# A half copy put behind all products of an up-projection tile, and accumulating transfers queued in threes

## The chip, the cores and the metric

The kernel runs on one core of one Trainium2 chip. The metric is the device time of one execution in microseconds. The kernel before took 2319.51 us (median of 3 runs, 2316.69 to 2325.53). All profile lines come from one further execution, which took 2328.08 us, 0.4% above that median.

## What is computed

A two-layer decoder trunk on one sequence of 256 rows of 2048 numbers, in float32. Each layer is a mixer (a short gated convolution, then stick-breaking attention) and an MLP, each with a norm before and after. The change lies in the MLP, which both layers have, with a hidden width of 8192:

```python
def sq_relu_mlp(u, w_up, w_down):
    return jnp.square(jax.nn.relu(u @ w_up)) @ w_down

for i in range(DEPTH):                       # DEPTH = 2
    ...
    u = rmsnorm(h, mlp_pre_g[i])
    h = h + rmsnorm(sq_relu_mlp(u, mlp_w_up[i], mlp_w_down[i]), mlp_post_g[i])
```

## The kernel before

**Two parts of each number.** The kernel's matmuls take operands of type float32r, so every float32 operand is split in two: a rounded high part (ScalarE, L163 or L208, tile `whi`) and what is left of it (VectorE, L174, tile `wlo`). A product of two numbers is made of three of the four products of the parts. Weights arrive in chunks of 128 x 1024 (512 KB) in four `raw` buffers (L147, issued by SyncE's queue), and the split parts lie in rings of seven `hi` and seven `lo` buffers. A `raw` buffer is loaded again when VectorE has made the low part of its chunk.

**The up projection.** A tile is 128 of the hidden columns for all 256 rows. It is summed in one PSUM bank of 512 columns. `high` (L899) makes 16 products of a weight's high part with both parts of `u`, 512 columns each: the first 256 columns of the bank hold high times high, the last 256 hold high times low. `half_of` (L910) then copies the last 256 columns to SBUF on ScalarE (L912, tile `half`). `low` (L914) makes 16 products of the weight's low part with the high part of `u`, 256 columns each, into the first 256 columns of the same bank. `finish` (L921) calls `Hidden.tile` (L857): VectorE adds `half` to the first 256 columns (L859, tile `s`), ScalarE takes relu and square (L860, L861), and the result is split for the next projection (L247/L248 or L842/L843).

**The order of the two projections.** The hidden width is cut into 8 steps of 8 tiles. `lead_up` (L924) makes the 8 tiles of the first step: six of them side by side, product by product, in banks 2 to 7, then two one after the other (`whole_up`, L946). From then on one tile of the next step (`whole_up`, always in bank 2, `UP_BANK`) takes turns with one pair of tiles of the down projection of this step (`Down.pair`, L1012). There are 56 such turns in each layer: 7 steps, each of two halves of four turns (m = 0 to 3).

**The down projection.** The pairs m = 1, 2, 3 of a half use a scheme with seven products in place of eight (`seven`, L1029: 21 matmuls of 512 columns, L1008 to L1010, in banks 3, 4, 5 and 6, 7, 0, 1). Its extra sums of weights are made by VectorE (L200) and of the hidden part by VectorE (L882). The pair m = 0 uses eight products (`eight`, L1040: 24 matmuls): first six into bank 3, six into bank 4, then six into bank 2, the bank of the up tile just before it, then six into bank 5. The bank-2 part is added to the result at once (L959 on ScalarE the first time, L961 on VectorE later), and the next up tile takes bank 2 again.

**Joints.** A `Down` object covers four turns at the start and eight turns after that, so there are seven joints in each layer at which one ends and the results leave PSUM: VectorE adds banks 3, 4 and 5 to the results (L961), and `add_later` (L965) copies banks 6, 7, 0 and 1 into a staging tile `more` (ScalarE, L969) and issues nine accumulating transfers of 256 KB each from SBUF to SBUF on GpSimd's queue (L975). Some of the nine depend on others: `r[0,1]`, `r[1,0]` and `r[1,1]` take several sums one after the other.

**What sets the order.** TensorE runs in the order of the code. A scheduler orders ScalarE, VectorE, GpSimd and SyncE by the program's order and its own estimate of when inputs are ready; each of these engines then runs strictly in that built order. `chunk` (L229) has weights split four chunks ahead of their use. Dependencies inside a PSUM bank are kept for the whole tile: a copy that reads the last 256 columns and a matmul that writes the first 256 are ordered one behind the other.

Of the kernel before, what the change touches and what calls it, by code (L numbers as in the profile page):

```python
# [9 lines left out]
F32 = mybir.dt.float32  # L10
F32R = mybir.dt.float32r
AF = mybir.ActivationFunctionType
ALU = mybir.AluOpType

P = 128
D = 2048
T = 256
NB = T // P
KD = D // P
# [67 lines left out]
def trunk(ctx, tc, x, xT, vecs, rows, ws, out):  # L87
    nc = tc.nc
# [30 lines left out]
    def bank(i, name):  # L119
        return psum.tile([P, 512], F32, tag=f"b{i}", name=name)  # L120
# [108 lines left out]
    def chunk(i, low=True):  # L229
        while count["split"] <= min(i + (AHEAD if i >= CALM else 2), len(stream) - 1, max(i, count["limit"])):  # L230
            split_one()
        if low:
            low_parts(i)
        return parts[i]
# [36 lines left out]
    def spent(us):  # L271
        clock["us"] += us
        while due and due[0][0] <= clock["us"]:
            heappop(due)[2]()
# [559 lines left out]
    def mlp(pool, i, before, after):  # L834
# [56 lines left out]
                two_parts(more, t[:, P:])  # L891
                return [one] + [[m[:, j * P : (j + 1) * P] for m in more] for j in range(3)]

        pss, halves = {}, {}

        def weight(part, first, m):
            return chunk(first + m // CH, part == 1)[part][:, m % CH * P : (m % CH + 1) * P]

        def high(first, m, k, n, number, b=None):  # L899

            if n not in pss:
                pss[n] = bank(number, "up")
            ps, x = pss[n][:].rearrange("p (a b t) -> p a b t", a=2, b=NB), u[k // 4][:, k % 4]
            if b is None:
                nc.tensor.matmul(ps, weight(0, first, m), x, start=k == 0, stop=k == KD - 1)  # L905
            else:
                nc.tensor.matmul(ps[:, :, b, :], weight(0, first, m), x[:, :, b, :], start=k == 0 and b == 0, stop=False)
            spent(TILE_HIGH if b is None else TILE_LOW)

        def half_of(n):  # L910
            halves[n] = pool.tile([P, T], F32, tag="half", name="half", bufs=2)
            nc.scalar.activation(halves[n][:], pss[n][:, T:], AF.Copy)  # L912

        def low(first, m, k, n):  # L914
            x = u[k // 4][:, k % 4, 0].rearrange("p b t -> p (b t)")
            nc.tensor.matmul(  # L916
                pss[n][:, :T], weight(1, first, m), x, start=False, stop=k == KD - 1, skip_group_check=True
            )
            spent(TILE_LOW)

        def finish(to, n):  # L921
            to.tile(n, pss.pop(n), halves.pop(n))

        def lead_up(to):  # L924
            first = W["mlp", i, 0].base
            place = {kn: m for m, kn in enumerate(UP_FIRST)}
            lead = list(range(LEAD_UP))
            alone = [(k, n) for k in range(ALONE) for n in lead]
            for b in range(NB):
                for k, n in sorted(alone, key=lambda kn: (kn[0] // 4, kn[1] // 3 if kn[0] < 4 else 0)):  # L930
                    high(first, place[k, n], k, n, n + 2, b)
            for k, n in alone:
                low(first, place[k, n], k, n)
            for k in range(ALONE, KD):
                for n in lead:
                    high(first, place[k, n], k, n, n + 2)
                for n in lead:
                    if k == KD - 1:
                        half_of(n)
                    low(first, place[k, n], k, n)  # L940
                    if k == KD - 1:
                        finish(to, n)
            for n in range(LEAD_UP, NF):
                whole_up(to, n, first + 2 * n, (n + 2) % 8)

        def whole_up(to, n, first, number):  # L946
            for k in range(KD):
                high(first, k, k, n, number)
            half_of(n)
            for k in range(KD):  # L950
                low(first, k, k, n)
            finish(to, n)
# [12 lines left out]
        def add_later(j, p1, p5, p6, p7):  # L965
            t = pool.tile([P, 4, 512], F32, tag="gpost", name="more", bufs=1)
            t1, t5, t6, t7 = (t[:, m, :] for m in range(4))
            for to, ps in ((t1, p1), (t6, p6), (t5, p5), (t7, p7)):
                nc.scalar.activation(to, ps[:], AF.Copy)  # L969
            r = {(b, c): part[b][2 * j + c] for b in range(NB) for c in range(2)}  # L970
            for to, more in (
                (t6, t1), (r[0, 0], t1), (r[0, 1], t5), (r[1, 0], t7), (r[1, 1], t5),
                (r[0, 1], t6), (r[1, 0], t6), (r[1, 1], t7), (r[1, 1], t6),
            ):
                nc.gpsimd.dma_start(to, more, accum_op=ALU.add)  # L975

        def add_now(j, p1, p5, p6, p7):
            w = pool.tile([P, 4, 512], F32, tag="gpre", name="more", bufs=1)
# [10 lines left out]
        class Down:  # L989
# [22 lines left out]
            def pair(self, at, first, xs):  # L1012
                e, m, _ = at
                seven = m in SEVEN[e][at[2]]
                (self.seven if seven else self.eight)(at, first, xs, 2 * m)
                if "more" in self.range and at == self.range["more"][1]:
                    ps = [self.ps.pop(n) for n in (1, 5, 6, 7)]
                    self.combine = lambda: (add_now if at[0] == STEPS - 1 else add_later)(self.j, *ps)
                    if at != self.plan[-1]:
                        self.combine()  # L1020
                        self.combine = None
                if at == self.plan[-1]:
                    last = e == STEPS - 1
                    for b, c in sorted(self.ps):
                        add(self.j, b, c, self.ps.pop((b, c)), last)
                    if self.combine:
                        self.combine()
# [27 lines left out]
        for e in range(STEPS):  # L1055
            for h in range(2):
                for m in SEVEN[e][h]:
                    n = 16 * h + 4 * m + 2 if e < STEPS - 1 else 8 * h + 2 * m
                    sevens[W["mlp", i, e + 1].base + n] = pool
        now = Hidden(0)  # L1060
        lead_up(now)
        for e in range(STEPS):
            first = W["mlp", i, e + 1].base
            if e == STEPS - 1:
                for b in range(NB):
                    scale[b] = small("hs")
                    nc.vector.tensor_tensor(scale[b][:], before.hs[b][:], before.hs[b][:], op=ALU.mult)
                after.gpost = row(pool, (B_MPOST0, B_MPOST1)[i], "gpost")
                turned["banks"] = [2, 3]
                for m in range(4):  # L1070
                    down.pair((e, m, 0), first + 2 * m, now)
                run(
                    [Group(first + 8, 8, now.xs, LAST_BANKS, lambda b, c, ps: add(band_of(e, 1), b, c, ps, True))],
                    leave=after,
                )
                break
            new = Hidden(e + 1)
            for h in range(2):
                if e == 0 or h == 1:
                    plan = [(e, m, h) for m in range(4)]  # L1080
                    if h == 1:
                        plan += [(e + 1, m, 0) for m in range(4)]
                    down = Down(band_of(e, h), plan)
                for m in range(4):
                    at_chunk = first + 16 * h + 4 * m
                    whole_up(new, 4 * h + m, at_chunk, UP_BANK)
                    down.pair((e, m, h), at_chunk + 2, now)
            now = new
# [7 lines left out]
    run(project(W["out"], y, 2, sublayer(mix0)), leave=mix0)  # L1096
    kv = KeyNorms(pool0, None)
    mlp(pool0, 0, mix0, kv)


# [169 lines left out]
    for j in range(4):  # L1270
        for i, (name, to, scale) in enumerate((
            ("k", kT, lambda b: kv.hs[b][:]), ("q", qT, lambda b: held["rq", b][:]),
        )):
            n = 2 * j + i
# [7 lines left out]

    pool1, mix1 = held["pool1"], held["mix1"]
    mlp(pool1, 1, mix1, OutNorms(pool1, None))
    pool1.release()

# [74 lines left out]
```

## Time and profile before

| what | us |
|---|---|
| median of 3 runs | 2319.51 |
| the profiled execution | 2328.08 |
| its span, first to last instruction | 2326.4 |
| TensorE busy | 2177.3 |
| VectorE busy | 1723.4 |
| ScalarE busy | 1381.2 |
| GpSimd busy | 116.4 |

The first MLP's 56 turns run from about 427 us to 1100 us of the span, the second's from about 1601 us to 2273 us. Rows of a timeline read: start, duration, engine (PE is TensorE's matmuls, DVE VectorE, ACT ScalarE, POOL GpSimd, SPq SyncE's queue), line of the kernel, operation, tiles, count, and in square brackets the idle time of that engine just before and what ended it. The wait rows give total time, number and longest. Matmuls overlap each other, so a row's duration is longer than the step from one matmul to the next.

### The profile page before, as it was taken

Reading aid. Unit: us, or ns where it says so; the run is one execution under the profiler, and the core shown is the slowest. Engines: PE = TensorE matmul, PEld = TensorE weight load, DVE = VectorE, ACT = ScalarE, POOL = GpSimd, SP = SyncE. Lnnn points to the kernel's source line nnn. Section 1 sums busy time; section 2 is a strip of 40 time slices with the busy share of each in tenths; the row PEclk is TensorE's granted clock in tenths of the full one; section 3 lists DMA queues with packets and bytes.
Section 4 is the critical chain, followed back from the end, with each engine's and each line's share of the span. In section 5 each row is a group of like instructions: output and inputs, shape, how many; then the busy total and the mean of one; then the engine's idle time right before and its main releaser. Section 6 shows DMA issues by size and latency. Waiting matters only on the chain.

```text
span 2326.4 us, 29793 instructions
## 1 busy us (share of the span) xinstructions
PE 2177.3 (94%) x10816; PEld 1824.8 (78%) x10816; DVE 1723.4 (74%) x2525; ACT 1381.2 (59%) x2108; POOL 116.4 (5%) x139
## 2 busy tenths in 40 slices
PE   9999998988989889999999999998898898989998
PEld 8888887777777777777888888886777777777777
DVE  8766647777877777888866777477777787877877
ACT  7554446555556555665568887456665565655654
POOL 0000000011010100101000000000100101001010
PEclk9999999999999999999999999999999999999999
DMA  8655664476575766757564455544766657666574
GB/s 307 202 188 189 228 193 160 141 211 189 184 211 190 201 193 188 219 190 222 175 223 154 163 179 200 183 157 147 215 183 211 195 186 208 192 210 197 179 231 145
DMA packets 132916, 450.28 MB, mean 194 GB/s; under 512 B 14880, under 2 KB 15136, under 8 KB 131744
## 3 DMA queue, kind: packets, MB, share of 16 engines
q1 hardware_dynamic: 113472, 408.65, 52.7%
q0 software_dynamic: 19008, 39.33, 8.9%
q8 instruction: 85, 1.39, 0.2%
q14 instruction: 63, 0.52, 0.1%
q10 hardware_dynamic: 288, 0.39, 0.0%
HBM read 413.19 MB, written 2.10 MB: 179 GB/s over the span
## 4 chain that ended last, share of the span: by engine, by line
PE 79%; DMA 8%; ACT 6%; DVE 4%; issue 2%; SPq 0%; DVEq 0%; ACTq 0%
PE up L905 15%; PE up L916 10%; PE acc L719 10%; DMA raw<-w_mlp 8%; PE acc L300 7%; PE acc L302 7%; PE acc L301 7%; PE acc L1008 4%; PE acc L1009 4%; PE acc L1010 4%; PE more L1008 3%; PE more L1009 3%; PE more L1010 3%; DVE wlo L174 2%; ACT half L912 2%
## 5 line engine op out<-in xcount | busy, mean ns | idle before, releaser
L174 DVE TENSOR_TENSOR wlo<-raw,whi 128x1024 fp32r<-128x1024 f32 (+1 forms) x506 | 606.7, 1208 | 246.7 <-ACT whi L163 171.4
L163 ACT ACTIVATE whi<-raw 128x1024 fp32r<-128x1024 f32 (+1 forms) x506 | 526.4, 1047 | 232.6 <-PE acc L302 84.0
L905 PE MATMUL up<-u,whi 128*128 128x512 f32 x1952 | 477.0, 397 | 18.0 <-DVE mg L961 9.2
L905 PEld LDWEIGHTS up<-u,whi 128*128 128x128 f32 x1952 | 373.4, 192 | 97.3 <-DVE mg L961 10.1
L916 PE MATMUL up<-u,wlo 128*128 128x256 f32 x2048 | 297.8, 299 | 120.8 <-ACT half L912 120.8
L916 PEld LDWEIGHTS up<-u,wlo 128*128 128x128 f32 x2048 | 269.0, 200 | 173.4 <-ACT half L912 172.2
L975 POOL DMA_DIRECT2D mg<-more x112 | 105.2, 1028 | 1475.1 <-ACT whi L163 682.8
L176 DVE SCALAR_TENSOR_TENSOR wlo<-raw,gv,whi 128x512 fp32r<-128x512 f32 (+1 forms) x160 | 132.0, 853 | 42.5 <-ACT whi L163 41.7
L719 PE MATMUL acc<-u,whi 128*128 128x512 f32 x672 | 156.5, 390 | 0.0
L300 PE MATMUL acc<-whi,u 128*128 128x512 f32 x384 | 153.1, 399 | 0.1
L163 ACT ACTIVATE whi<-raw,gv 128x512 fp32r<-128x512 f32 (+1 forms) x160 | 121.7, 800 | 51.0 <-PE acc L302 38.6
L302 PE MATMUL acc<-whi,u 128*128 128x512 f32 x384 | 149.9, 390 | 0.0
L301 PE MATMUL acc<-wlo,u 128*128 128x512 f32 x384 | 149.8, 390 | 0.0
L860 ACT ACTIVATE s<-s 128x256 f32<-128x256 f32 x128 | 52.5, 412 | 158.1 <-DVE s L859 157.8
L719 PEld LDWEIGHTS acc<-u,whi 128*128 128x128 f32 x672 | 124.8, 188 | 25.0
L200 DVE TENSOR_TENSOR sums<-raw,sums 128x512 f32<-128x512 f32 x172 | 117.9, 685 | 1.6
L200 DVE TENSOR_TENSOR sums<-raw,raw 128x512 f32<-128x512 f32 x86 | 58.9, 685 | 49.3 <-DMA raw<-w_mlp 49.3
L719 PEld LDWEIGHTS acc<-u,wlo 128*128 128x128 f32 x672 | 83.5, 192 | 1.7
L912 ACT ACTIVATE half<-up 128x256 f32<-128x256 f32 x128 | 48.2, 380 | 61.6 <-PE up L905 61.5
L302 PEld LDWEIGHTS acc<-whi,u 128*128 128x128 f32 x384 | 72.1, 188 | 15.6
L719 PE MATMUL acc<-u,wlo 128*128 128x256 f32 x672 | 84.2, 283 | 0.0
L1008 PE MATMUL acc<-whi,hid 128*128 128x512 f32 x204 | 83.4, 409 | 0.0
(4467 smaller groups left out, 4069.9 us busy)
## 6 DMA issues: line engine op xcount, KB each, us to landing
raw<-w_mlp SPq DMA_DIRECT2D x512, 512.0 KB, 4.3
raw<-w_in SPq DMA_DIRECT2D x94, 512.0 KB, 3.9
mg<-more POOLq DMA_DIRECT2D x112, 256.0 KB, 6.5
raw<-w_out SPq DMA_DIRECT2D x32, 512.0 KB, 3.6
raw<-w_v SPq DMA_DIRECT2D x32, 512.0 KB, 4.4
raw<-w_k SPq DMA_DIRECT2D x32, 512.0 KB, 4.3
raw<-w_q SPq DMA_DIRECT2D x32, 512.0 KB, 4.2
raw<-w_wo SPq DMA_DIRECT2D x32, 512.0 KB, 3.6
```

The costliest lines, as they stand in the source:

```text
L163: rounded = nc.scalar.activation(hi[:, at], raw[i][:, at], AF.Copy, scale=1.0 if gain is None else gain)
L174: nc.vector.tensor_tensor(lo[:, at], t[:, at], hi[:, at].bitcast(F32), op=ALU.subtract)
L200: nc.vector.tensor_tensor(t, x, y, op=ALU.subtract)
L300: nc.tensor.matmul(ps[:], xh, hi[:, a], start=i == 0 and k == 0, stop=False)
L301: nc.tensor.matmul(ps[:], xh, lo[:, a], start=False, stop=False)
L302: nc.tensor.matmul(ps[:], xl, hi[:, a], start=False, stop=i == self.n - 1 and k == self.ks - 1)
L719: nc.tensor.matmul(ps[:, :cols], w, xs[:, :cols], start=k == 0 and part == parts[0], stop=k == KD - 1 and part == parts[1], skip_group_che ...
L905: nc.tensor.matmul(ps, weight(0, first, m), x, start=k == 0, stop=k == KD - 1)
L916: nc.tensor.matmul(pss[n][:, :T], weight(1, first, m), x, start=False, stop=k == KD - 1, skip_group_check=True)
L1008: nc.tensor.matmul(self.ps[key][:], xh, hi, start=first, stop=False)
L1009: nc.tensor.matmul(self.ps[key][:], xh, lo, start=False, stop=False)
L1010: nc.tensor.matmul(self.ps[key][:], xl, hi, start=False, stop=last)
```

## The change

```diff
-        pss, halves = {}, {}
+        pss, adds = {}, []
...
-                nc.tensor.matmul(ps, weight(0, first, m), x, start=k == 0, stop=k == KD - 1)
+                nc.tensor.matmul(ps, weight(0, first, m), x, start=k == 0, stop=False)
...
-        def half_of(n):
-            halves[n] = pool.tile([P, T], F32, tag="half", name="half", bufs=2)
-            nc.scalar.activation(halves[n][:], pss[n][:, T:], AF.Copy)
-
         def low(first, m, k, n):
             x = u[k // 4][:, k % 4, 0].rearrange("p b t -> p (b t)")
-            nc.tensor.matmul(
-                pss[n][:, :T], weight(1, first, m), x, start=False, stop=k == KD - 1, skip_group_check=True
-            )
+            nc.tensor.matmul(pss[n][:, :T], weight(1, first, m), x, start=False, stop=k == KD - 1)
             spent(TILE_LOW)

         def finish(to, n):
-            to.tile(n, pss.pop(n), halves.pop(n))
+            ps, half = pss.pop(n), pool.tile([P, T], F32, tag="half", name="half", bufs=2)
+            copied = nc.scalar.activation(half[:], ps[:, T:], AF.Copy)
+            to.tile(n, ps, half)
+            for a, more in adds[:3]:
+                with tc.issue_after(copied.ins):
+                    nc.gpsimd.dma_start(a, more, accum_op=ALU.add)
+            del adds[:3]
...
                 for n in lead:
-                    if k == KD - 1:
-                        half_of(n)
                     low(first, place[k, n], k, n)
...
             for k in range(KD):
                 high(first, k, k, n, number)
-            half_of(n)
             for k in range(KD):
                 low(first, k, k, n)
             finish(to, n)
...
-            for to, more in (
+            adds.extend((
                 (t6, t1), (r[0, 0], t1), (r[0, 1], t5), (r[1, 0], t7), (r[1, 1], t5),
                 (r[0, 1], t6), (r[1, 0], t6), (r[1, 1], t7), (r[1, 1], t6),
-            ):
-                nc.gpsimd.dma_start(to, more, accum_op=ALU.add)
+            ))
```

The half copy of a tile is now made after its 32 products, in `finish` (L917 of the changed kernel). The nine transfers of a joint are put in a list, and each `finish` that follows issues up to three of them, inside `tc.issue_after` of that tile's half copy. Other lines move up by 3 or 4: the adds L959 and L961 become L956 and L958, the staging copy L969 becomes L966, and the transfers L975 become L921.

## The prediction

> **What bounds the kernel now.** I read the page first, for who is busy and who waits, then TensorE's waits, then timelines of single tiles, and last the built order of the changed kernel's instructions.
>
> ```profile
> span 2326.4 us, 29793 instructions
> PE 2177.3 (94%) x10816; PEld 1824.8 (78%) x10816; DVE 1723.4 (74%) x2525; ACT 1381.2 (59%) x2108; POOL 116.4 (5%) x139
> L174 DVE TENSOR_TENSOR wlo<-raw,whi 128x1024 fp32r<-128x1024 f32 (+1 forms) x506 | 606.7, 1208 | 246.7 <-ACT whi L163 171.4
> L163 ACT ACTIVATE whi<-raw 128x1024 fp32r<-128x1024 f32 (+1 forms) x506 | 526.4, 1047 | 232.6 <-PE acc L302 84.0
> L916 PE MATMUL up<-u,wlo 128*128 128x256 f32 x2048 | 297.8, 299 | 120.8 <-ACT half L912 120.8
> L912 ACT ACTIVATE half<-up 128x256 f32<-128x256 f32 x128 | 48.2, 380 | 61.6 <-PE up L905 61.5
> ```
>
> ```profile
> PE up L916 <- ACT half L912: 120.8, 124, 5.2
> PE up L905 <- DVE mg L961: 9.2, 2, 4.7
> PE up L905 <- ACT mg L959: 8.8, 2, 4.8
> ```
>
> TensorE is the bound, and nearly all its idle time, 120.8 + 18.0 = 138.8 us, lies in the up projection: 124 of 128 tiles make it wait between `high` and `low` for the half copy. That wait is exactly what the change takes out of the order. What a wait costs is seen in the timeline of two tiles, the first before a pair of 21 products, the second before one of 24:
>
> ```profile
> 607.93 3.79 PE L905 MATMUL up<-u,whi 128*128 128x512 f32 x16
> 612.19 2.17 PE L916 MATMUL up<-u,wlo 128*128 128x256 f32 x16 [0.47 <-ACT half L912]
> 614.20 0.40 PE L1008 MATMUL more<-whi206a,hid 128*128 128x512 f32 x1
> ...
> 618.99 3.79 PE L905 MATMUL up<-u,whi 128*128 128x512 f32 x16
> 624.07 2.18 PE L916 MATMUL up<-u,wlo 128*128 128x256 f32 x16 [1.29 <-ACT half L912]
> 626.08 0.40 PE L1008 MATMUL acc<-whi,hid 128*128 128x512 f32 x1
> ...
> 631.55 3.79 PE L905 MATMUL up<-u,whi 128*128 128x512 f32 x16
> ```
>
> By starts: 21 products step from 614.20 to 618.99, 4.79 us (0.228 each); 24 from 626.08 to 631.55, 5.47; 16 lows take 614.20 - 612.19 = 2.01; 16 highs at 0.228 are 3.64. So a tile needs 5.65 us. The first tile's lows would start at 611.57 and start at 612.19: a wait of 0.47 costs 0.62. The second costs 1.44.
>
> **What all waits cost.** From the lows of the first turn's tile to those of the 56th, and from the last six highs of the leading tiles to that same first row, in both layers:
>
> ```profile
> 396.52 1.55 PE L905 MATMUL up<-u,whi 128*128 128x512 f32 x6
> 426.82 2.17 PE L916 MATMUL up<-u,wlo 128*128 128x256 f32 x16 [0.52 <-ACT half L912]
> 1095.38 2.17 PE L916 MATMUL up<-u,wlo 128*128 128x256 f32 x16 [0.47 <-ACT half L912]
> 1571.10 1.55 PE L905 MATMUL up<-u,whi 128*128 128x512 f32 x6
> 1600.87 2.17 PE L916 MATMUL up<-u,wlo 128*128 128x256 f32 x16 [0.52 <-ACT half L912]
> 2268.27 2.17 PE L916 MATMUL up<-u,wlo 128*128 128x256 f32 x16 [0.47 <-ACT half L912]
> ```
>
> Between the first two marks of a layer's turns lie 55 tiles, 41 pairs of 21 and 14 of 24: 55 x 5.65 + 41 x 4.79 + 14 x 5.47 = 583.7. They took 668.6 and 667.4, so 84.9 + 83.7 are lost. Ahead of them lie six highs, six lows, two tiles and 16 highs: 1.37 + 0.75 + 11.30 + 3.64 = 17.1; they took 30.3 and 29.8, so 13.2 + 12.7 are lost. **Together 194.5 us**: the 138.8 of idle time, 124 x 0.15 = 19 in the overlap of matmuls, and some 37 of products at half rate behind long waits.
>
> **The joints.** The long waits come once per `Down` object, 14 times. A layer's third joint:
>
> ```profile
> 664.73 3.79 PE L905 MATMUL up<-u,whi 128*128 128x512 f32 x16
> 665.17 0.33 SPq L147 DMA_DIRECT2D raw<-w_mlp  x1
> 665.32 2.35 POOL L975 DMA_DIRECT2D mg<-more  x2
> 672.06 0.69 DVE L200 TENSOR_TENSOR sums<-raw,raw 128x512 f32<-128x512 f32 x1 [2.61 <-DMA raw<-w_mlp]
> 672.12 1.06 ACT L208 ACTIVATE whi230b<-raw 128x1024 fp32r<-128x1024 f32 x1 [4.33 <-DMA raw<-w_mlp]
> 673.08 0.37 ACT L912 ACTIVATE half<-up 128x256 f32<-128x256 f32 x1
> 673.50 3.78 PE L916 MATMUL up<-u,wlo 128*128 128x256 f32 x16 [4.99 <-ACT half L912]
> 677.39 0.42 DVE L859 TENSOR_TENSOR s<-up,half 128x256 f32<-128x256 f32 x1 [2.83 <-PE up L916]
> ```
>
> The load issued at 665.17, beside the accumulating transfers, lands 6.9 us later; the page gives 4.3 as the median:
>
> ```profile
> raw<-w_mlp SPq DMA_DIRECT2D x512, 512.0 KB, 4.3
> mg<-more POOLq DMA_DIRECT2D x112, 256.0 KB, 6.5
> ```
>
> ScalarE waits for it with the half copy next in its queue, and TensorE waits for the copy. Price: 4.99 + 0.15, and the lows then take 3.78 instead of 2.17, so 6.8; with a few slow products behind, 7. At the first two joints of a layer the wait stands ahead of the highs (bank 2, released by L959 or L961) and costs about 7.6. So the joints hold 14 x 7.1 = 99 us of the 194.5, the plain waits 95.
>
> **Part 1, the copy behind the lows.** No instruction is added or dropped; 128 copies of 380 ns move. In the changed order `low` waits only for weights, so the 95 us go if the new place delays nobody. What is queued behind: on VectorE `s`, now behind the copy; on TensorE the next use of bank 2, which needs copy (0.38) and `s` (0.42) after the lows. Before a pair of 21 there are 4.79 us for that 0.8, before a pair of 24 the 12 products into banks 3 and 4, 2.73 us, so there is room for one split ahead of each (1.05 on ScalarE, 1.21 on VectorE): 3.1 in the first case, and in the second the built order has only such splits ahead as can run before the lows end. I take nothing for plain tiles. For the leading tiles the copies fall behind TensorE's next 11.3 us of tiles; nothing there needs their banks sooner.
>
> At a joint the block on ScalarE stays, but TensorE runs on. With the load landing at 672.06 as now: lows end at 664.73 + 5.65 = 670.38; twelve products until 673.1; then bank 2. The copy is done at 673.45; on VectorE two L200 (0.6 apart) and a half-size split come ahead of `s`, which ends near 674.3: a wait of 1.2. The six products into bank 2 and the next six end at 677.0; the add that frees bank 2 (0.69) stands in the built order behind `s`, one L200, two splits and a small operation, about 3.1 us, and ends near 678.1: a wait of 1.1. So 2.3 of idle time per joint, and perhaps the half rate. Two rows say what that takes:
>
> ```profile
> 2182.30 3.33 PE L916 MATMUL up<-u,wlo 128*128 128x256 f32 x16 [1.79 <-ACT half L912]
> 966.08 2.17 PE L916 MATMUL up<-u,wlo 128*128 128x256 f32 x16 [3.43 <-ACT half L912]
> ```
>
> A wait of 1.79 was followed by slow lows (1.16 more), one of 3.43 was not. I take 1.2 per joint for it: 3.5 in all, between 0 and the present 7.1. [...]
>
> **Part 2, three transfers per tile.** `issue_after` orders only instructions of the copy's own engine, and the transfers are GpSimd's. In the built order they stand together as before and wait for the staging copies, the adds and one another, none for a half copy. So I take nothing: GpSimd will still issue them at a joint as its inputs come. If they were held, a load beside three of them would lie between 4.3 and 6.9 us; at 4.3, issued at 665.17, it lands at 669.5, and the joint's 3.5 us go.
>
> **Sum.** 194.5 - 14 x 3.5 = 145.5 us less. The profiled execution of 2328.1 would become 2182.6; it is 8.6 above the median, so the median becomes 2319.5 - 145.5 = **2174 us**.
>
> **Rivals.**
>
> *A, joints cost less.* [...] For: the built order issues some loads sooner at the joint, since a split moves ahead of an add. Against: 2182.30.
>
> *B, VectorE or the joints take part of it back.* One stretch between joints:
>
> ```profile
> 646.87:743.54 96.67, 87.88 (x430) 73.10 (x430) 76.02 (x108) 56.76 (x87) 7.93 (x9) 0.96 0.65 199
> DVE sums L200 <- DMA raw<-w_mlp: 61.2, 31, 6.2
> ```
>
> TensorE needs 8 x 5.65 + 6 x 4.79 + 2 x 5.47 = 84.9 us for it. VectorE (third busy figure) is busy 76.0, waits 61.2 / 14 = 4.4 for loads, and would wait about 0.5 for each of eight copies: 84.4. There is no room left; if its other waits stay, a stretch takes some 91.5, and the gain is 5.2 x 14 + 26 = 99: 2221. Joints that keep their 7.1 give the same, 2319.5 - 95 = 2224. Against: many of VectorE's waits are for a TensorE that would come earlier.
>
> *C, slower: bank 2.* If copy and `s` regularly end more than 4.8 us after the lows, since splits that wait for loads stand ahead of them, every one of 112 tiles waits for its bank. It decides from 194.5 / 112 = 1.74 us beyond that slack; at 2.0 beyond, 2319.5 + 30 = 2349. For: the release now goes through two queues in series. Against: it takes three splits ahead on each engine, and now the longest such delays are at 14 joints only.
>
> *D, the change does what it says*, transfers held in threes: A's lower end, 2125 to 2150.
>
> **Chances.** Forecast (2160 to 2200) 0.42; A with D (2125 to 2160) 0.26; B (2200 to 2230) 0.21; more taken back, still faster, 0.04; no change 0.02; C 0.05. A measurement of this kernel tells about 0.5% (11.6 us) from no change. Faster by more than that 0.93, within it 0.02, slower 0.05. The range 2133 to 2230 holds the forecast and most of A and B.
>
> **What would show it.** Right: the wait of L916's successor (L912) for the half copy gone from TensorE's waits; a pair of 21 and its tile in 10.44 us between starts; at joints short waits of L1004 and L905's highs for VectorE; GpSimd's nine transfers within some 20 us of each joint. Wrong: TensorE waiting for `wlo` or `whi` in plain turns (B); highs waiting for `s` at every tile (C); the transfers spread over three tiles (D).

## The result, and the profile after

| | before | after |
|---|---|---|
| median, us | 2321.07 (2316.69 to 2325.53, 4 runs) | 2153.82 (2151.56 to 2158.07, 4 runs) |
| the profiled execution, us | 2328.08 | 2151.56 |
| its span, us | 2326.4 | 2149.4 |

The median of the kernel before holds one run more than the 2319.51 that stood ahead of the prediction. The ratio is 0.9281, 95% interval 0.9258 to 0.9305: 167 us less by the medians, 176.5 between the two profiled executions. The time lies in the range on record (2133 to 2230) and 20 us under the forecast of 2174.

The page of the changed kernel, the lines that answer to those of before (lows are now L912, the half copy L917):

```profile
PE 2121.2 (99%) x10816; PEld 1804.9 (84%) x10816; DVE 1708.3 (79%) x2525; ACT 1386.8 (65%) x2108; POOL 116.2 (5%) x139
L174 DVE TENSOR_TENSOR wlo<-raw,whi 128x1024 fp32r<-128x1024 f32 (+1 forms) x506 | 605.4, 1208 | 200.7 <-ACT whi L163 142.8
L912 PE MATMUL up<-u,wlo 128*128 128x256 f32 x2048 | 268.0, 283 | 0.0
L917 ACT ACTIVATE half<-up 128x256 f32<-128x256 f32 x128 | 47.5, 378 | 75.4 <-PE up L912 75.3
```

The copies still cost ScalarE the same (47.5 us against 48.2), and the lows have no idle time ahead of them at all, where 120.8 us stood. TensorE's waits:

```profile
PE more L1004 <- DVE s L859: 12.9, 12, 2.2
PE up L905 <- DVE mg L958: 4.1, 7, 0.7
PE up L905 <- DVE s L859: 0.6, 1, 0.6
```

Of 138.8 us of idle time in the up projection and behind it, 17.6 are left in this execution, and they now stand where bank 2 is used next. The same marks as in the prediction, in the timeline of the changed kernel: in each layer the last six highs of the leading tiles, the lows of the first turn's tile, those of the 56th:

```profile
396.83 1.55 PE L905 MATMUL up<-u,whi 128*128 128x512 f32 x6
413.72 2.08 PE L912 MATMUL up<-u,wlo 128*128 128x256 f32 x16
1004.80 2.08 PE L912 MATMUL up<-u,wlo 128*128 128x256 f32 x16
1480.56 1.55 PE L905 MATMUL up<-u,whi 128*128 128x512 f32 x6
1497.44 2.08 PE L912 MATMUL up<-u,wlo 128*128 128x256 f32 x16
2091.40 2.08 PE L912 MATMUL up<-u,wlo 128*128 128x256 f32 x16
```

The leading tiles take 16.9 us in both layers (30.3 and 29.8 before), the turns 591.1 and 594.0 (668.6 and 667.4). So 13.4 + 12.9 + 77.5 + 73.4 = 177.2 us went, which is the whole difference of the two profiled executions: on balance nothing outside these stretches moved. What is left to gain there follows from a plain turn:

```profile
595.94 3.79 PE L905 MATMUL up<-u,whi 128*128 128x512 f32 x16
...
606.27 3.79 PE L905 MATMUL up<-u,whi 128*128 128x512 f32 x16
609.89 2.08 PE L912 MATMUL up<-u,wlo 128*128 128x256 f32 x16
611.80 0.40 PE L1004 MATMUL more<-whi218a,hid 128*128 128x512 f32 x1
```

Start to start it takes 10.33 us; 16 highs take 3.63 as before, but the lows 611.80 - 609.89 = 1.91, not the 2.01 that they took behind a wait. Without any wait a layer's 55 tiles and pairs would need 55 x 5.54 + 41 x 4.79 + 14 x 5.47 = 577.7, so 13.4 + 16.3 = **29.7 us are left**. That is the figure of one execution, the shortest of four. By the same marks two further profiled executions of the same program, e1 and e11 below, leave 37 and 41 us, and their waits for bank 2 sum to 23.9 and 24.2 us where this one has 17.6.

### The profile page after: what moved, and what is told of

Read it like the earlier page. It is cut to its first block, busy times and chain, and to the rows that moved or that the text cites. A ratio compares the mean times of both kernels' runs of the same rounds, so it can differ in the third digit from the quotient of the medians.

```text
span 2149.4 us, 29843 instructions
## 1 busy us (share of the span) xinstructions
PE 2121.2 (99%) x10816; PEld 1804.9 (84%) x10816; DVE 1708.3 (79%) x2525; ACT 1386.8 (65%) x2108; POOL 116.2 (5%) x139
## 4 chain that ended last, share of the span: by engine, by line
PE 84%; DVE 8%; DMA 5%; issue 2%; ACT 1%; SPq 0%; DVEq 0%; ACTq 0%
PE up L905 17%; PE acc L719 11%; PE up L912 9%; PE acc L300 7%; PE acc L301 7%; PE acc L302 7%; DMA raw<-w_mlp 5%; PE more L1004 4%; PE more L1005 3%; PE more L1006 3%; PE acc L1004 3%; PE acc L1005 3%; PE acc L1006 3%; DVE wlo L174 2%; DVE sums L200 2%
## 5 line engine op out<-in xcount | busy, mean ns | idle before, releaser
L174 DVE TENSOR_TENSOR wlo<-raw,whi 128x1024 fp32r<-128x1024 f32 (+1 forms) x506 | 605.4, 1208 | 200.7 <-ACT whi L163 142.8
L905 PE MATMUL up<-u,whi 128*128 128x512 f32 x1952 | 466.8, 390 | 4.7 <-DVE mg L958 4.1
L905 PEld LDWEIGHTS up<-u,whi 128*128 128x128 f32 x1952 | 364.7, 188 | 83.7 <-DVE mg L958 7.5
L912 PEld LDWEIGHTS up<-u,wlo 128*128 128x128 f32 x2048 | 263.6, 191 | 10.3
L912 PE MATMUL up<-u,wlo 128*128 128x256 f32 x2048 | 268.0, 283 | 0.0
L921 POOL DMA_DIRECT2D mg<-more x112 | 100.5, 997 | 1310.6 <-ACT s L860 573.8
L200 DVE TENSOR_TENSOR sums<-raw,sums 128x512 f32<-128x512 f32 x172 | 117.9, 685 | 1.4
L200 DVE TENSOR_TENSOR sums<-raw,raw 128x512 f32<-128x512 f32 x86 | 59.2, 689 | 48.1 <-DMA raw<-w_mlp 47.5
L917 ACT ACTIVATE half<-up 128x256 f32<-128x256 f32 x128 | 47.5, 378 | 75.4 <-PE up L912 75.3
L302 PEld LDWEIGHTS acc<-whi,u 128*128 128x128 f32 x384 | 72.1, 188 | 15.5
L300 PEld LDWEIGHTS acc<-whi,u 128*128 128x128 f32 x384 | 72.2, 188 | 14.0 <-ACT tk L1194 0.7
```

The source lines that it names most:

```text
L174: nc.vector.tensor_tensor(lo[:, at], t[:, at], hi[:, at].bitcast(F32), op=ALU.subtract)
L200: nc.vector.tensor_tensor(t, x, y, op=ALU.subtract)
L300: nc.tensor.matmul(ps[:], xh, hi[:, a], start=i == 0 and k == 0, stop=False)
L302: nc.tensor.matmul(ps[:], xl, hi[:, a], start=False, stop=i == self.n - 1 and k == self.ks - 1)
L912: nc.tensor.matmul(pss[n][:, :T], weight(1, first, m), x, start=False, stop=k == KD - 1)
```

## The experiments

The same program's median lay between 2153.8 and 2161.5 us on different occasions (the changed kernel, e1 and e11), so a difference under some 8 us tells nothing unless the two were measured together; e1 to e4 were, e5 to e8, and e9 to e11.

### Each part alone (e1, e2)

e1 keeps the new place of the copy and issues the nine transfers in a loop, as before:

```diff
-            for a, more in adds[:3]:
-                with tc.issue_after(copied.ins):
-                    nc.gpsimd.dma_start(a, more, accum_op=ALU.add)
-            del adds[:3]
...
-            adds.extend((
+            for to, more in (
...
-            ))
+            ):
+                nc.gpsimd.dma_start(to, more, accum_op=ALU.add)
```

> The half copy behind the lows as in the change, the nine transfers of a joint queued at once as before. The built order of every engine is that of the changed kernel. Theory (the whole gain is the moved copy; the threes order nothing): the time of the changed kernel, 2154 us within 6. Rival (queuing in threes gives part of the gain): at least 12 us more, 2166 or above.

Measured: 2160.08 us, ratio 0.9307 (0.9278 to 0.9335). In the traces every engine runs the changed kernel's instructions in the changed kernel's order. The difference to 2153.82 is therefore spread between occasions.

e2 keeps the copy between highs and lows and queues the transfers in threes, in each tile's `finish`, without `issue_after`:

> The copy between highs and lows as before, the transfers handed out three per tile. Theory: the time of the kernel before, 2321 us within 6, and the transfers of a joint stand as close together as before (five within 6 us). Rival: the transfers spread over three tiles, the 14 waits of about 4.4 us at the joints shrink, 2300 or below.

Measured: 2324.0 us, ratio 1.0009 (0.9987 to 1.0031). Every engine's order is that of the kernel before, and so is TensorE's wait:

```profile
PE up L916 <- ACT half L912: 119.6, 124, 5.8
```

The gain is part 1's alone. Part 2 leaves no mark on the program.

### Transfers truly held back (e3)

A one-column copy of `half` on GpSimd stands ahead of each three transfers, so that they can't start before that tile's half copy:

```diff
+                mark = pool.tile([P, 1], F32, tag="mark", name="mark", bufs=2)
+                held_back = nc.gpsimd.tensor_copy(mark[:], half[:, 0:1])
                 for a, more in adds[:3]:
-                    with tc.issue_after(copied.ins):
+                    with tc.issue_after(held_back.ins):
```

> The changed kernel, but each group of three transfers stands on GpSimd's queue behind a one-column copy that reads the tile's half, so the groups are held until their tile's half copy is done. Theory (what is left at the joints is the order of VectorE's work, not the transfers): 2154 us within 8, the 17.6 us of waits for bank 2 between 10 and 20. Rival D (spacing relieves the loads): the waits at joints go, 2140 or below.

Measured: 2162.43 us, ratio 0.9309 (0.9278 to 0.9341), beside e1's 2160.08. GpSimd's timeline at a layer's third joint, first of the changed kernel, then of e3:

```profile
625.26 0.87 POOL L921 DMA_DIRECT2D mg<-more  x1 [66.08 <-ACT s L860]
626.91 0.87 POOL L921 DMA_DIRECT2D more<-more  x1 [0.78 <-ACT hid L247]
627.90 2.67 POOL L921 DMA_DIRECT2D mg<-more  x3
```

```profile
632.53 0.21 POOL L921 COPY mark<-half 128x1 f32<-128x1 f32 x1 [57.13 <-ACT half L917]
...
643.53 0.64 POOL L921 COPY mark<-half 128x1 f32<-128x1 f32 x1 [7.74 <-ACT half L917]
...
654.79 0.19 POOL L921 COPY mark<-half 128x1 f32<-128x1 f32 x1 [8.01 <-ACT half L917]
```

In the changed kernel five transfers are issued between 625.26 and 630.57; the half copy of the tile that hands them out runs only at 634.16 (shown further below), so `issue_after` held none of them for it. In e3 they stand in three groups, 11 us apart, behind such a copy. It brings nothing: TensorE's waits for bank 2 are 26.4 us, two of them 0.5 in all beside those shown, and e1's are 23.9.

```profile
PE more L1007 <- DVE s L859: 20.6, 12, 2.4
PE up L905 <- DVE s L859: 5.3, 10, 1.0
```

VectorE's waits for loads are no shorter either: 64.6 us at L200, where the changed kernel has 63.9. Why spacing relieves no load, no run here shows.

### Without the transfers (e4, e5)

e4 is the changed kernel without the 126 transfers, e5 the kernel before without them; the sums that they make are left out.

```diff
-            for a, more in adds[:3]:
-                with tc.issue_after(copied.ins):
-                    nc.gpsimd.dma_start(a, more, accum_op=ALU.add)
-            del adds[:3]
+            del adds[:]
```

> The changed kernel with the 126 accumulating transfers left out, so the sums they carry are missing from the output. It bounds what any spacing of them can give. Theory: the waits for bank 2 at joints shrink by at most half, those in the middle of a stretch stay: 2142 to 2152. Rival (the transfers slow the loads and so cause all that is left): 2137 or below.

> The kernel before with the 126 accumulating transfers left out, so the sums they carry are missing from the output. Theory (the 14 long waits at joints, 7.1 us each, come from loads that land late beside the transfers): most of 14 x 5.5 = 77 us goes, 2235 to 2265, and no wait of TensorE at a joint is above 2.5 us. Rival (the long waits come from the extra copies and adds of a joint on ScalarE and VectorE): 2300 or above, waits over 3 us stay.

Measured: e4 2125.96 us, ratio 0.9155 (0.9129 to 0.9181), 34 under e1, which was measured together with it, and 28 under the first median of the changed kernel. My theory gave 2142 to 2152 and fell; the rival was right. TensorE's waits in e4:

```profile
PE more L1001 <- DVE s L859: 0.5, 1, 0.5
```

So nearly all of what the changed kernel leaves over hangs on the transfers: by the same marks the turns of e4 lose 3.7 us where the changed kernel loses 29.7. They act through the loads, as VectorE's waits for them show, in the changed kernel and then in e4; no VectorE, ScalarE or TensorE instruction of the changed kernel is listed as waiting for a transfer itself.

```profile
DVE sums L200 <- DMA raw<-w_mlp: 63.9, 61, 2.8
```

```profile
DVE sums L200 <- DMA raw<-w_mlp: 13.1, 23, 1.4
```

e5: 2267.66 us, ratio 0.9765 (0.9736 to 0.9794), 2 us above the expected range, which ended at 2265. Its waits between highs and lows, and the split ahead of the half copy on ScalarE at a layer's third joint:

```profile
PE up L916 <- ACT half L912: 98.5, 124, 3.2
```

```profile
654.51 1.06 ACT L208 ACTIVATE whi230b<-raw 128x1024 fp32r<-128x1024 f32 x1 [1.51 <-DMA raw<-w_mlp]
```

The longest fell from 5.2 to 3.2 (3.1 at a joint, where 2.5 at most was expected), and the two groups of waits of L905 for bank 2 (18.0 together) are gone. At this joint the split L208 waited 4.33 for its load in the kernel before and 1.51 here. So of the 99 us that the prediction put at the joints of before the transfers carried some 55, by the medians. What stays is the copy waiting its turn on ScalarE behind the joint's other work, part of which still waits for a load, now with no transfer beside it.

### Which tiles carry the gain (e6, e7)

The copy goes back between highs and lows for the 28 tiles ahead of a pair m = 0 (e6), or for the 84 ahead of m = 1, 2, 3 (e7), and nowhere else:

```diff
+            early = half_of(n) if number == UP_BANK and n % 4 == 0 else None
             for k in range(KD):
                 low(first, k, k, n)
-            finish(to, n)
+            finish(to, n, early)
```

> The changed kernel with the copy put back between highs and lows for the 28 tiles m = 0 alone. Theory: these tiles hold the 14 joints (7.1 us each where the wait is at the lows) and 14 waits of about 1.2 in mid stretch; some 14 x 5.8 + 14 x 0.8 = 92 us come back: 2225 to 2255. Rival (every tile's wait weighs about the same, 1.5 us each): 28 x 1.5 = 42, about 2196.

> The changed kernel with the copy put back for the 84 tiles m = 1 to 3 alone. Theory: each costs the plain 0.62 us, 52 us come back: 2200 to 2212. Rival (1.5 us each): 126 us, about 2280. Second rival (the joints' waits come back with them): 2230 or above.

Measured: e6 2225.15 us, ratio 0.9588 (0.9564 to 0.9613), 71 above the changed kernel's first median, at the low edge; e7 2233.84 us, ratio 0.9624 (0.9588 to 0.9659), 80 above, where the theory gave 2200 to 2212; the second rival, that the joints' waits come back, was right. With the leading tiles' 26 the two make 177, where the medians of before and after lie 167 apart. Why e7 missed stands in its waits, below that of e6:

```profile
PE up L912 <- ACT half L917: 59.8, 28, 4.4
```

```profile
PE up L912 <- ACT half L917: 40.7, 84, 1.3
PE up L905 <- DVE mg L963: 13.9, 10, 5.2
...
PE up L905 <- ACT mg L961: 7.4, 2, 4.3
```

The copy of a plain tile costs what was reckoned (40.7 / 84 = 0.48 of idle time each). But with plain tiles slow again, the long waits at the first two joints of each layer come back too: 3.1 to 5.2 ahead of the highs, 16.2 together, though no copy ahead of a pair m = 0 was moved. In e6 no wait ahead of the highs is longer than 1.9. So the waits at these four of the 14 joints, which the prediction priced as joints, go with the order of the plain tiles.

### Trying to win the rest (e8 to e12)

e8 gives the half copy and `s` a high priority in the scheduler:

```diff
-                nc.vector.tensor_tensor(s[:], ps[:, :T], half[:], op=ALU.add)
+                with tc.high_priority():
+                    nc.vector.tensor_tensor(s[:], ps[:, :T], half[:], op=ALU.add)
...
-            copied = nc.scalar.activation(half[:], ps[:, T:], AF.Copy)
+            with tc.high_priority():
+                copied = nc.scalar.activation(half[:], ps[:, T:], AF.Copy)
```

> The changed kernel with the half copy and the addition s put ahead of other ready work by the scheduler. Theory (what is left are waits for bank 2 behind other work on VectorE, 12.9 us for s and 4.7 at the highs): up to 12 us less, 2142 to 2154, with the wait for s gone. Rival (blocking the queues for s makes splits late): 2160 or above, with waits for wlo or whi.

Measured: 2158.61 us, ratio 0.93 (0.9276 to 0.9324): no gain that can be told, and 4.6 us above the theory's range. The waits for `s`, which the theory had gone, are 17.9 us. The order hardly changed: 72 of ScalarE's 2108 instructions and 82 of VectorE's 2525 stand at another place.

e9 replaces the nine transfers by nine additions on GpSimd:

```diff
-            for a, more in adds[:3]:
-                with tc.issue_after(copied.ins):
-                    nc.gpsimd.dma_start(a, more, accum_op=ALU.add)
-            del adds[:3]
+            for a, more in adds:
+                nc.gpsimd.tensor_tensor(a, a, more, op=ALU.add)
+            del adds[:]
```

> The changed kernel with the nine accumulating transfers of a joint replaced by nine additions on GpSimd, in SBUF. Theory (what is left above 2126 us is the transfers' share of the DMA engines, and GpSimd is idle): 2122 to 2140, TensorE's waits for bank 2 under 3 us. Rival (GpSimd's additions slow VectorE's work or end too late): 2154 or above, with longer VectorE instructions or waits for GpSimd.

Measured: 2262.1 us, ratio 0.9751 (0.9735 to 0.9766), 101 above e11, measured together with it; the rival, that GpSimd's additions slow VectorE's work, was right. TensorE now waits longer for `s`, and some of VectorE's small sums take much longer than the others (count, then shortest, median and longest in ns):

```profile
PE more L1003 <- DVE s L859: 104.5, 16, 7.7
```

```profile
L882 DVE TENSOR_TENSOR sq<-sq,s x44: 277/285/1382, 409.1 to 2138.0; 128x128 f32<-128x128 f32 x44
```

```profile
642.96 10.45 POOL L920 TENSOR_TENSOR mg<-mg,more 128x512 f32<-128x512 f32 x7 [1.06 <-ACT more L965]
644.55 1.38 DVE L882 TENSOR_TENSOR sq<-sq,s 128x128 f32<-128x128 f32 x1
```

An operation of 285 ns takes 1382 inside GpSimd's chain of additions, some 1.5 us each: 1.1 us more, most of one addition. In the changed kernel none of these 44 takes over 293 ns. How the one engine holds up the other, no run here shows. VectorE is busy 1834.4 us in all, 126 more than in the changed kernel.

e10 makes eight transfers of nine by using a sum twice (`t7` takes `t6`, and `r[1,0]` then takes `t7` alone); e11 is the changed kernel again:

```diff
-                (t6, t1), (r[0, 0], t1), (r[0, 1], t5), (r[1, 0], t7), (r[1, 1], t5),
-                (r[0, 1], t6), (r[1, 0], t6), (r[1, 1], t7), (r[1, 1], t6),
+                (t6, t1), (r[0, 0], t1), (r[0, 1], t5), (t7, t6), (r[1, 1], t5),
+                (r[0, 1], t6), (r[1, 0], t7), (r[1, 1], t7),
```

> The changed kernel with eight transfers per joint in place of nine (one sum is made first and used twice). Theory (the cost goes with the transferred bytes, some 28 us for nine): about 3 us less, 2148 to 2156, not to be told from no change for sure. Rival (the length of the chain of transfers counts): 2160 or above.

> The changed kernel once more, beside the others on the same chip. Theory: 2154 to 2160; this tells how far the 2160 of the kernel with the moved copy alone is from it.

Measured: e10 2154.0 us, ratio 0.928 (0.9263 to 0.9296); e11 2161.45 us, ratio 0.9311 (0.9293 to 0.9328). The intervals just overlap; a gain of some 7 us is likely, not certain.

e12 makes two of the staged sums on their way out of PSUM, on VectorE in place of ScalarE's copies, and so needs six transfers:

```diff
-            for to, ps in ((t1, p1), (t6, p6), (t5, p5), (t7, p7)):
+            for to, ps in ((t1, p1), (t5, p5)):
                 nc.scalar.activation(to, ps[:], AF.Copy)
+            for to, more, ps in ((t6, t1, p6), (t7, t6, p7)):
+                nc.vector.tensor_tensor(to, more, ps[:], op=ALU.add)
...
-                (t6, t1), (r[0, 0], t1), (r[0, 1], t5), (r[1, 0], t7), (r[1, 1], t5),
-                (r[0, 1], t6), (r[1, 0], t6), (r[1, 1], t7), (r[1, 1], t6),
+                (r[0, 0], t1), (r[0, 1], t5), (r[1, 1], t5), (r[0, 1], t6), (r[1, 0], t7), (r[1, 1], t7),
```

> The changed kernel with six transfers per joint: two of the staged sums are made by VectorE straight from PSUM in place of two of ScalarE's copies, and each serves several results. Theory (the transfers cost some 30 us in all and the cost goes with their number): 30 x 3 / 9 = 10 us less, against 14 x 1.4 = 20 us of VectorE work that counts only where VectorE is the last at a joint: 2140 to 2156. Rival (VectorE's work decides at the joints): 2164 or above, with longer waits for s.

Measured: **2137.82 us**, ratio 0.9207 (0.9189 to 0.9226), better than both kernels and 2 us below the expected range; the rival of 2164 or above fell. The interval lies below that of e11 (0.9293 to 0.9328) and of the changed kernel (0.9258 to 0.9305).

```profile
PE more L1005 <- DVE s L859: 6.2, 9, 1.5
```

The waits for `s` fall to 6.2, from 12.9 to 18.5 in the changed kernel's three profiled executions. With none (e4), six (e12), eight (e10) and nine transfers (e1, e11) the times are 2126, 2138, 2154 and 2160 to 2161: it is faster with fewer, where their spacing (e3) did nothing. But by its number e12 should have gained a third of e4's 34 us, 11, and it gained 16 to 24. It also moves two copies from ScalarE to VectorE and shortens the chain of transfers that wait for one another, and neither was tried apart.

## Why the prediction was right, and where its sizes were off

**Mechanism: right.** The wait for the half copy is gone from TensorE's list, the copies hide behind TensorE's next products, and part 2 does nothing, as the prediction had it (e1, e2). A pair of 21 and its tile take 10.33 us between starts, where 10.44 was the sign to look for. The leading tiles gave their 26 us, and e6 and e7 share the rest out among the turns.

**The joints' 3.5 us: too dear.** 14 x 3.5 = 49 us were to stay. 29.7 stayed in the profiled execution, which makes this the term that was mis-sized most; 37 and 41 stayed in e1 and e11. The joint that the prediction worked out, in the timeline of the changed kernel, with the issue of the load that it waits for:

```profile
626.48 0.33 SPq L147 DMA_DIRECT2D raw<-w_mlp  x1
626.92 3.79 PE L905 MATMUL up<-u,whi 128*128 128x512 f32 x16
633.13 0.69 DVE L200 TENSOR_TENSOR sums<-raw,raw 128x512 f32<-128x512 f32 x1 [1.60 <-DMA raw<-w_mlp]
634.16 0.37 ACT L917 ACTIVATE half<-up 128x256 f32<-128x256 f32 x1
634.95 0.41 DVE L859 TENSOR_TENSOR s<-up,half 128x256 f32<-128x256 f32 x1
635.41 0.19 PEld L1004 LDWEIGHTS more<-whi,hid 128*128 128x128 f32 x1 [0.47 <-DVE s L859]
638.35 0.68 DVE L958 TENSOR_TENSOR mg<-mg,more 128x512 f32<-128x512 f32 x1
639.08 1.20 PE L905 MATMUL up<-u,whi 128*128 128x512 f32 x4 [0.64 <-DVE mg L958]
```

Counted from the highs' start, VectorE has its load at 6.2 us where I had kept the 7.33 of before; `s` ends at 8.4 (9.6), and the add that frees bank 2 at 12.1 (13.4). So this joint has next to no wait for `s`, where 1.2 was reckoned (a weight load waits 0.47, behind the products still running), and 0.64 for bank 2, where it was 1.1. The load takes nearly as long as before, 6.65 us from issue to use against 6.89. But it is issued 0.44 us ahead of the highs, where the one of before was issued 0.44 behind their start. I had held the landing fixed at its time of before, though I noted under rival A that some loads would be issued sooner. That is where this term went wrong.

**The half rate: it came seldom.** 1.2 per joint was the guess, 16.8 in all. In the turns of the profiled execution the granted clock is at half for two stretches of 3.41 us only, behind the two waits of 2.23 us. A stretch at half speed loses half of its length, so this cost some 3.4 us. With 17.6 of idle time and some 3 in the overlap of 20 waits that makes 24 of the 29.7. Of the rest 2.2 us lie in the first step behind each of the 20 waits, which takes 0.34 us where 0.23 is usual (462.79 to 463.12, in the last section, is one).

**Waits away from joints: left out.** I took nothing for plain turns. By their place in the order six of the twelve waits of L1004 for `s` belong to turns m = 0 in the middle of a stretch, 3.8 us together. That is small, and in e4, without the transfers, one wait of 0.5 is left of all twelve.

**The lows: 0.1 us too slow.** I took 2.01 us for 16 lows from rows behind a wait. Without one they take 1.91, so the turns gained 2 x 6.0 = 12.0 us more than reckoned.

**The sum.** 49 - 29.7 = 19.3 and 12.0 make 31.3 more than the 145.5, so 176.8, as measured between the profiled executions. By the medians (2319.5 at the prediction, 2153.8 measured) the gain is 11 smaller, since the profiled execution of before was 8.6 above its median and that of after 2.3 below; so the time is 20 and not 31 under the forecast. That part of the error is hidden in this way is luck; with e1's or e11's time the forecast's own bounds (2160 to 2200) would just have held.

**The rivals.** 2153.8 lies in A's interval (2125 to 2160), six under the forecast's; e1 and e11 lie on the border between them. What spoke for A came true: the load at the third joint was issued sooner and landed 1.1 us earlier against the highs (6.2 us after their start, 7.33 before), and slow products grew rare, two stretches of 3.41 us. The bounds of A were my estimate, and that a joint's waits leave the clock at full speed was not shown: behind the two of 2.23 us it was halved. B fell. VectorE is busy 89 of 100 us in the stretch (third busy figure), more than before, and TensorE is still the bound:

```profile
600.00:700.00 100.00, 99.31 (x509) 84.33 (x508) 89.21 (x126) 67.27 (x101) 7.90 (x9) 1.00 0.74 220
```

As the prediction's "against" had it, part of VectorE's waits were for work that comes earlier now: its idle time ahead of L174 fell from 246.7 to 200.7 us. Its waits for loads (L200) stayed, 63.9 us against 61.2. C fell: no turn away from a joint waits for bank 2 by more than 1.1 us. D fell twice: the transfers aren't held (the changed kernel), and holding them gives nothing (e3).

## What to carry to other kernels

A wait of half a microsecond between two halves of one accumulation counts once for each tile, 124 times here; where nothing between the halves needs the copy, put it behind the last product and look only at who needs the bank next. When a wait goes, don't carry the other engines' times of before over: what stood in the queue behind it, loads above all, moves earlier too. Before a traffic jam is spread out, leave the traffic out once: here spacing the transfers gave nothing, and the version with six in place of nine, which also moves two copies, gave 16 to 24 us that no reordering did.

## What the runs showed of the hardware

- Behind the two waits of 2.23 us in the changed kernel TensorE's products ran at full speed for 1.2 and 1.3 us more and only then at half speed. One of them in its timeline:

```profile
462.79 0.50 PE L1004 MATMUL more<-whi,hid 128*128 128x512 f32 x1 [2.23 <-DVE s L859]
463.12 0.40 PE L1005 MATMUL more<-wlo,hid 128*128 128x512 f32 x1
463.36 0.39 PE L1006 MATMUL more<-whi,hid 128*128 128x512 f32 x1
...
464.47 0.63 PE L1004 MATMUL acc<-whi,hid 128*128 128x512 f32 x1
464.90 0.63 PE L1005 MATMUL acc<-wlo,hid 128*128 128x512 f32 x1
```

  The step is 0.24 us before and 0.43 after. The wait of 3.43 in the kernel before, though longer, left no mark on the products behind it (0.23 a step from 968.10 on).

  In these traces it goes by where the gap falls. In both, the stretches at half clock start at whole multiples of 3.41 us from one another. The stretches of that length, cut at these marks, around the gaps, the changed kernel's first, then that of the 3.43 and that of the 1.79 of the kernel before (TensorE's busy time is the first busy figure, the granted clock stands before the last two):

```profile
460.63:464.04 3.41, 1.25 (x5) 1.05 (x6) 3.41 (x6) 1.15 (x3) 1.74 (x2) 1.00 0.94 260
464.04:467.46 3.42, 3.42 (x10) 2.62 (x8) 1.75 (x4) 1.84 (x3) 0.87 (x1) 0.50 1.03 286
```

```profile
960.90:964.31 3.41, 1.75 (x8) 1.13 (x6) 2.68 (x4) 1.03 (x3) 0.89 (x1) 1.00 1.07 268
964.31:967.72 3.41, 1.64 (x13) 1.64 (x14) 2.50 (x4) 2.33 (x3) 0.87 (x1) 1.00 1.07 247
2179.46:2182.87 3.41, 1.62 (x9) 1.12 (x8) 2.40 (x5) 2.31 (x5) 0.00 (x0) 1.00 0.81 316
```

  The gap of 3.43 lies across two of them, and TensorE is busy for 1.75 and 1.64 us; full clock follows both. The gaps of 2.23 and 1.79 fall into one each, with 1.25 and 1.62 us busy, and half clock follows. In the traces of the two kernels half clock followed all 21 such stretches at full clock in which TensorE was busy for 1.63 us or less, and none of those in which it was busy for 1.64 or more.
- 16 lows took 0.1 us more behind a wait (2.01, kernel before) than straight after highs (1.91, changed kernel).
- Nine transfers of 256 KB per joint, 126 in all, cost 28 to 34 us in the changed kernel (e4) and 55 in the one before (e5). The loads beside them land later: at a layer's third joint one of 512 KB took 6.9 us from issue to use in the kernel before and 4.1 in e5 (issued at 650.37, used at 654.51), and VectorE's waits for loads at L200 are 63.9 us in the changed kernel and 13.1 in e4.
